# Two-layer hybrid encoder on one core: the low parts of seven split weights move from GpSimd to VectorE

## The chip, the core and the metric

The kernel runs on one core of a Trainium2 chip. A core has TensorE (PE in the profile, with PEld for its weight loads), VectorE (DVE), ScalarE (ACT), GpSimd (POOL), a queue that issues transfers (SP), and sixteen DMA engines. The metric is the device time of one execution in microseconds. The kernel before took 1442.82 us, the median of three runs (1442.33 to 1444.71).

## The reference

The input x has 256 tokens of 1024 channels in float32. After a first layer norm come two layers. Each is a mixer (one input projection, eight heads of neighbourhood attention, eight heads of sliding-window attention with two key heads and sink logits, sigmoid gates, an output projection), a residual and a layer norm, and then a channel part, a residual and a layer norm:

```
x = layer_norm(x, emb_ln_g, emb_ln_b)
for layer in range(DEPTH):
    m = mixer_block(x, w_in[layer], ...)
    x = layer_norm(DEEPNORM_ALPHA * x + m, ln1_g[layer], ln1_b[layer])
    f = swiglu(x, ...) if layer % 2 == 0 else moe_swiglu(x, w_router, ...)
    x = layer_norm(DEEPNORM_ALPHA * x + f, ln2_g[layer], ln2_b[layer])
```

The channel part of layer 0 is a dense SwiGLU of width 2816. That of layer 1 sends each token to 2 of 8 experts of width 3584.

## The kernel before

Everything up to the experts is done in three matmuls for one product: a float32 operand is split into a high part, rounded to the fp32r type, and a low part, the rest. `mm3` (L201) then adds hi·hi, hi·lo and lo·hi; these are the lines L203 to L205. Weights are split as they arrive: `load_w` (L167) transfers 128x2048 numbers (1 MB; for the first projection of a layer, `wkv`, 128x1024) into a `raw` tile, ScalarE copies them to `hi` (L185), and one engine subtracts, `lo = raw - hi` (L192). That engine is `dve`, unless the list `splitters` holds an entry, which is then used up: `eng = splitters.pop() if splitters else dve`.

The activations are split where one layer norm feeds the next product. I call such a place a meeting. There are three of them before the experts:

- the first: the embedding norm feeds the mixer of layer 0 (0 to 45 us of the trace);
- the second: the first norm of layer 0 feeds the dense SwiGLU (180 to 210 us);
- the third: the second norm of layer 0 feeds the mixer of layer 1 (380 to 412 us).

At a meeting the two halves of 128 tokens, t = 0 and t = 1, are done one after the other. VectorE adds the residual (L280), takes the statistics (L216, L217), and normalises (L224, L225). TensorE transposes (L255). ScalarE and VectorE scale half of the channels each into `xTf` (L265, L263). VectorE rounds to `xTh` (L272, two casts of 128x512) and subtracts to `xTl` (L273, two of 128x512). The matmuls of the next product then start on t = 0, and the transposes of t = 1 stand among them (`rest`). Meanwhile GpSimd works on the residual copy of x: `ln_apply` multiplies each half by the norm's gain (L234, 128x1024) once its transposes have been read, and adds the bias (L237).

The order of the instructions on each engine is set when the kernel is built, by a scheduler that estimates times, except in the stretches marked `manual_schedule`, which keep the order of the code. So a changed engine for one instruction can also change the order around it. The experts, from 594 us on, stream 896 KB and 1 MB pieces of unsplit weights into all free weight tiles (`rooms`), so transfers run ahead until the rooms are full.

Of the kernel before, what the change touches and what calls it, by code (L numbers as in the profile page):

```python
# [65 lines left out]
def tile_encoder(ctx: ExitStack, tc: tile.TileContext, x_in, emb_g, emb_b, w_in, b_gate, na_rpb, sw_sink,  # L66
# [3 lines left out]
    pe, act, dve, pool = nc.tensor, nc.scalar, nc.vector, nc.gpsimd  # L70
# [9 lines left out]
    def mm_bank():  # L80
        return pp.tile([128, 512], F32, tag="mm", name="mm")
# [61 lines left out]
    splitters = []  # L143
# [58 lines left out]
    def mm3(o, lh, ll, rh, rl, first, last):  # L202
        pe.matmul(o, lh, rh, start=first, stop=False)  # L203
        pe.matmul(o, lh, rl, start=False, stop=False)  # L204
        pe.matmul(o, ll, rh, start=False, stop=last)  # L205
# [80 lines left out]
    def mixer(l, xh, xl, rest, x, mp, close_attention, early):  # L286
# [9 lines left out]
        def load_cols(c0, n):  # L296
            return [load_w(win[:, kh * 4:kh * 4 + 4, c0:c0 + n], 4, n) for kh in range(2)]
# [39 lines left out]
        def ev_vna(t, ps):  # L337
            return act.activation(vna[:, t].rearrange("p h d -> p (h d)"), ps, AF.Copy)

        splitters[:] = [pool] * 3 if l else [pool,pool]  # L340
        wkv = load_cols(2048, 256)
        if l == 0:
            with tc.manual_schedule(engines={PE, ACT, DVE}):
# [229 lines left out]
    def dense_ffn(x, xh, xl, rest, fp, early):  # L573
# [6 lines left out]
        def load_gu(j):  # L580
            return [load_w(w[:, :, j * 256:(j + 1) * 256], 8, 256) for w in (wg, wu)]

        def new_h():
            return (fp.tile([128, 2, S], F32R, name="hh", bufs=4), fp.tile([128, 2, S], F32R, name="hl", bufs=4))

        def first():

            splitters[:] = [pool] * 2
            ws = load_gu(0)
            hh, hl = new_h()  # L590
            hts = []
            for t in range(2):
                tk = slice(t * 128, (t + 1) * 128)
                ps = mm_bank().rearrange("p (b s) -> p b s", b=2)
                for b, (wh, wl) in enumerate(ws):
                    with ExitStack() as es:
                        for c in range(KC):
                            if (t, b, c) == (0, 1, 2):
                                es.enter_context(tc.manual_schedule(engines={PE}))
                                out = rest()  # L600
                            mm3(ps[:, b], xh[:, c, tk], xl[:, c, tk], wh[:, c], wl[:, c], c == 0, c == 7)
                h = fp.tile([128, S], F32, name="h", bufs=3)
                with tc.issue_after(out.ins):
                    act.activation(h, ps[:, 0], AF.Silu)
                dve.tensor_mul(h, h, ps[:, 1])
                hts.append(h)
            yield hh, hl
            for t, h in enumerate(hts):
                tk = slice(t * 128, (t + 1) * 128)
                ps = mm_bank().rearrange("p (m s) -> p m s", m=4)[:, 0:2]  # L610
                for m in range(2):
                    pe.transpose(ps[:, m], h[:, m * 128:(m + 1) * 128], ident)
                act.activation(hh[:, :, tk], ps, AF.Copy)
                dve.tensor_sub(hl[:, :, tk], ps, hh[:, :, tk])
            yield
# [28 lines left out]


        steps = first()
        hs = [next(steps)]
        for j in range(1, NJ):
# [28 lines left out]
    def rest(ln, g, b):  # L677
        def part():
            out = to_xT(xt, ln, 1, *xT)
            if ln == 0:  # L680
                return lambda: ln_apply(xt, bcast(g, nc.sync), b, pool)
            hold_back(0, *out)
            ln_apply(xt, bcast(g), b, pool)
            return out[0]
        return part
# [9 lines left out]
    with tc.tile_pool(name="mix0", bufs=1) as mp:  # L695
        mixer(0, *xT, rest(0, emb_g, emb_b), xt, mp, lambda ap: pools["att0"].close(), early(1))
# [76 lines left out]
    with tc.tile_pool(name="mix1", bufs=1, reuse_waits="tile") as mp:  # L773
        mixer(1, *xT, rest(2, ln2_g[0], ln2_b[0]), xt, mp, prefetch_room, routed)
# [426 lines left out]
```

## Time and profile before

| | before |
|---|---|
| median of three runs | 1442.82 us (1442.33 to 1444.71) |
| the profiled execution | 1444.1 us, of it 1442.2 us span |
| PE busy | 1383.3 us, 96% |
| VectorE busy | 513.5 us, 36% |
| ScalarE busy | 336.3 us, 23% |
| GpSimd busy | 125.5 us, 9% |
| mean granted TensorE clock | 0.985 of full speed |
| transfers | 451.24 MB, 313 GB/s over the span |

A row of the timeline has the start in us, the duration in us, the engine, the line of the kernel, the operation, what it writes and reads with the shape, the count of like instructions in a row, and in brackets the idle time before it and what ended that. The duration of an instruction here includes time in which it has been started and stands still. The granted clock is given as a share of 2.4 GHz: 1.00 is 2.4 GHz and 0.50 is 1.2 GHz.

### The profile page before, as it was taken

What the parts mean: (1) busy time and instruction counts of PE and PEld (TensorE: products, weight loads), DVE (VectorE), ACT (ScalarE), POOL (GpSimd) and SP (SyncE); (2) the same over time, 40 slices, a digit from 0 to 9 for tenths busy, and PEclk for the clock granted to TensorE, in tenths of its full rate; (3) what the DMA queues carried; (4) which work ended last, traced back from release to release, by engine and by line L of the source; (5) the groups of instructions that cost most, each with busy time, mean ns of one, the idle gap of its engine ahead of it and who ended that gap; (6) DMA issues with size and microseconds to landing.
All of it is one profiled execution on the core that took longest, in us unless ns stands there. A gap on an engine that the chain in (4) does not pass through costs nothing. (4 is left out here: it accounts for less than half of the span.)

```text
span 1442.2 us, 26993 instructions
## 1 busy us (share of the span) xinstructions
PE 1383.3 (96%) x11875; PEld 777.2 (54%) x11875; DVE 513.5 (36%) x661; ACT 336.3 (23%) x533; POOL 125.5 (9%) x71
## 2 busy tenths in 40 slices
PE   7999989999899999899999999999999999999974
PEld 5888979999788898332333333333323233333321
DVE  8675676445687746710111201102010111101113
ACT  4566444444355662200000000000000000000000
POOL 5210051000351100500000000000000000000000
PEclk8999999999999999999999999999999999999998
DMA  8734437565466387599999999999999999999993
GB/s 288 238 117 153 154 125 245 179 190 166 142 202 180 104 339 253 207 419 419 418 405 364 366 419 418 419 419 417 419 419 419 419 419 417 420 419 418 418 420 145
DMA packets 122858, 451.24 MB, mean 313 GB/s; under 512 B 8032, under 2 KB 57568, under 8 KB 108528
## 3 DMA queue, kind: packets, MB, share of 16 engines
q1 hardware_dynamic: 120768, 442.91, 79.0%
q0 software_dynamic: 1968, 6.55, 1.5%
q8 instruction: 95, 1.56, 0.4%
q14 instruction: 27, 0.22, 0.0%
HBM read 448.38 MB, written 1.05 MB: 312 GB/s over the span
## 5 line engine op out<-in xcount | busy, mean ns | idle before, releaser
L933 PE MATMUL mm<-raw,gx 128*32 128x448 f32 x3648 | 370.4, 540 | 1.9 <-DMA raw<-in_moe_w_up_dram 1.3
L933 PEld LDWEIGHTS mm<-raw,gx 128*32 128x32 f32 x3648 | 117.1, 110 | 226.0 <-issue 209.6
L192 DVE TENSOR_TENSOR lo<-raw,hi 128x2048 fp32r<-128x2048 f32 x78 | 191.7, 2464 | 89.8 <-ACT hi L185 89.6
L962 PE MATMUL a<-raw,hT 128*32 128x512 f32 x1680 | 197.5, 594 | 11.3 <-DMA raw<-in_moe_w_down_dram 11.3
L203 PE MATMUL mm<-xTh,hi 128*128 128x256 f32 x704 | 202.3, 287 | 0.0
L205 PE MATMUL mm<-xTh,lo 128*128 128x256 f32 x704 | 200.0, 284 | 0.0
L204 PE MATMUL mm<-xTl,hi 128*128 128x256 f32 x704 | 199.7, 284 | 0.0
L933 PE MATMUL a<-raw,gx 128*32 128x448 f32 x1728 | 187.4, 540 | 0.0
L185 ACT ACTIVATE hi<-raw 128x2048 fp32r<-128x2048 f32 (+1 forms) x85 | 158.7, 1873 | 74.4 <-PE mm L204 43.2
L203 PEld LDWEIGHTS mm<-xTh,hi 128*128 128x128 f32 x704 | 134.6, 191 | 7.2 <-issue 5.4
L205 PEld LDWEIGHTS mm<-xTh,lo 128*128 128x128 f32 x704 | 134.6, 191 | 3.1 <-issue 3.1
L204 PEld LDWEIGHTS mm<-xTl,hi 128*128 128x128 f32 x704 | 134.7, 191 | 1.8 <-issue 1.5
L938 DVE TENSOR_TENSOR h<-h,mm 128x448 f32<-128x448 f32 x32 | 19.9, 621 | 304.6 <-PE mm L933 302.0
L962 PEld LDWEIGHTS a<-raw,hT 128*32 128x32 f32 x1680 | 50.8, 110 | 135.4 <-issue 102.6
L933 PEld LDWEIGHTS a<-raw,gx 128*32 128x32 f32 x1728 | 55.4, 110 | 107.6 <-issue 102.9
L937 ACT ACTIVATE h<-mm 128x448 f32<-128x448 f32 x25 | 13.6, 544 | 320.1 <-PE mm L933 320.1
L967 PE MATMUL a<-raw,hT 128*32 128x512 f32 x560 | 72.8, 592 | 0.0
L945 DVE STREAM_TRANSPOSE hT<-h 128x1344 f32<-128x1344 f32 (+1 forms) x15 | 33.6, 2239 | 105.5 <-PE a L967 54.0
L1116 POOL DMA_DIRECT2D raw<-in_ln_g_dram x1 | 0.6, 602 | 774.7 <-PE mm L933 774.7
L976 ACT ACTIVATE y<-a 128x512 f32<-128x512 f32 x8 | 4.8, 597 | 270.9 <-PE a L962 270.9
L205 PE MATMUL mm<-hi,xTl 128*128 128x256 f32 (+1 forms) x128 | 46.6, 365 | 6.8 <-DVE xTl L273 6.8
L203 PE MATMUL mm<-hi,xTh 128*128 128x256 f32 (+1 forms) x128 | 46.4, 367 | 3.8 <-DVE xTh L272 3.8
(244 smaller groups left out, 1463.8 us busy)
## 6 DMA issues: line engine op xcount, KB each, us to landing
raw<-in_moe_w_gate_dram SPq DMA_DIRECT2D x128, 896.0 KB, 17.8
raw<-in_moe_w_up_dram SPq DMA_DIRECT2D x128, 896.0 KB, 17.4
raw<-in_moe_w_down_dram SPq DMA_DIRECT2D x111, 1024.0 KB, 18.5
raw<-in_w_in_dram SPq DMA_DIRECT2D x32, 1024.0 KB, 5.8
raw<-in_ffn_w_gate_dram SPq DMA_DIRECT2D x11, 1024.0 KB, 5.3
raw<-in_ffn_w_up_dram SPq DMA_DIRECT2D x11, 1024.0 KB, 5.4
raw<-in_ffn_w_down_dram SPq DMA_DIRECT2D x11, 1024.0 KB, 5.0
raw<-in_w_out_dram SPq DMA_DIRECT2D x8, 1024.0 KB, 5.6
```

What stands on the lines that cost most here:

```text
L185: act.activation(hi[:, p], raw[:, p], AF.Copy)
L192: eng.tensor_sub(lo[:, p], raw[:, p], hi[:, p])
L203: pe.matmul(o, lh, rh, start=first, stop=False)
L204: pe.matmul(o, lh, rl, start=False, stop=False)
L205: pe.matmul(o, ll, rh, start=False, stop=last)
L933: pe.matmul(out[q * 32:q * 32 + 32], gx[:, c, s * 32:s * 32 + 32], wt[:, q * Q:(q + 1) * Q], start=c == 0, stop=c == KC - 1)
L937: act.activation(h[:, s, 0:Q], banks[0][s], AF.Silu)
L938: dve.tensor_mul(h[:, s, 0:Q], h[:, s, 0:Q], banks[1][s])
L945: dve.transpose(hT, h.rearrange("p s (f b) -> p s b f", f=32))
L962: pe.matmul(yb[0][r:r + 32], hT[s][:, m], w[:, n * 512:(n + 1) * 512], start=first, stop=last)
L967: pe.matmul(yb[1][r:r + 32], hT[2][:, m - 1 + i], wt[:, i, n * 512:(n + 1) * 512], start=j == 0 and m == 1, stop=last)
L976: act.activation(y[:, 0], yb[0], AF.Copy)
```

## The change

The two places that fill the list `splitters` now empty it. So all low parts are made by VectorE. Before, GpSimd made two of them at the first meeting (`wkv`, 128x1024 each), two at the second (the first gate and up weights of the dense SwiGLU, 128x2048), and three at the third (`wkv` twice 128x1024, and the first half of `wq`, 128x2048).

```
@@ -337,7 +337,7 @@
         def ev_vna(t, ps):
             return act.activation(vna[:, t].rearrange("p h d -> p (h d)"), ps, AF.Copy)
 
-        splitters[:] = [pool] * 3 if l else [pool,pool]
+        splitters.clear()
         wkv = load_cols(2048, 256)
         if l == 0:
             with tc.manual_schedule(engines={PE, ACT, DVE}):
@@ -585,7 +585,7 @@
 
         def first():
 
-            splitters[:] = [pool] * 2
+            splitters.clear()
             ws = load_gu(0)
             hh, hl = new_h()
             hts = []
```

GpSimd keeps its other work in its old order. On VectorE the seven subtractions take the following places. At the first meeting (181 and 187 are the two halves of `wkv`, `xTf_138` and `xTf_128` belong to t = 0, `bnrs_118` to the norm of t = 1):

```order
 L263 TENSOR_SCALAR xTf_138<-mm_133,pcol_79 128x128 x4
+L192 TENSOR_TENSOR lo_181<-raw_178,hi_180 128x1024
 L224 RECIPROCAL bnrs_118<-bnrs_118 128x1
 L225 TENSOR_SCALAR x_76<-x_76,bnmv_117,bnrs_118 128x1024
 L272 CAST xTh_99<-xTf_128 128x4x128
+L192 TENSOR_TENSOR lo_187<-raw_184,hi_186 128x1024
 L273 TENSOR_TENSOR xTl_100<-xTf_128,xTh_99 128x4x128
 L272 CAST xTh_99<-xTf_138 128x4x128
```

Two subtractions now stand between the scaling of t = 0 and its first low part.

At the second meeting the subtraction of the gate weights stands ahead of the first residual sum of t = 0 (L280). That of the up weights, 1955, is this one (1896 and 1886 are the two scaled halves of t = 0):

```order
 L216 BN_STATS bnst_1928<-x_76 128x6
 L263 TENSOR_SCALAR xTf_1896<-mm_1891,pcol_79 128x128 x4
+L192 TENSOR_TENSOR lo_1955<-raw_1952,hi_1954 128x2048
 L272 CAST xTh_1879<-xTf_1896 128x4x128
 L272 CAST xTh_1879<-xTf_1886 128x4x128
```

It stands between the scaling of t = 0 and its two casts.

At the third meeting (3746 and 3752 are the halves of `wkv`, 3665 and 3655 the scaled halves of t = 0):

```order
 L224 RECIPROCAL bnrs_3615<-bnrs_3615 128x1
 L225 TENSOR_SCALAR x_76<-x_76,bnmv_3614,bnrs_3615 128x1024
+L192 TENSOR_TENSOR lo_3746<-raw_3743,hi_3745 128x1024
 L263 TENSOR_SCALAR xTf_3665<-mm_3660,pcol_79 128x128 x4
+L192 TENSOR_TENSOR lo_3752<-raw_3749,hi_3751 128x1024
 L272 CAST xTh_3648<-xTf_3665 128x4x128
 L272 CAST xTh_3648<-xTf_3655 128x4x128
```

One stands ahead of the scaling of t = 0, which waits for the transposes, the other ahead of its casts.

A little later on VectorE (3758 is the first half of `wq`, `a2` and `a3` are the two residual sums of t = 1):

```order
 L273 TENSOR_TENSOR xTl_3649<-xTf_3655,xTh_3648 128x4x128
 L280 SCALAR_TENSOR_TENSOR x_76<-x_76,a2_1944 128x512
+L192 TENSOR_TENSOR lo_3758<-raw_3755,hi_3757 128x2048
 L216 BN_STATS bnst_3704<-x_76 128x6
 L280 SCALAR_TENSOR_TENSOR x_76<-x_76,a3_1945 128x512
```

This one stands inside the residual and norm of t = 1.

TensorE's order at the same place (3768 is the product with `wkv`, 3795 that with `wq`, both of t = 0; L255 are the transposes of t = 1):

```order
 L204 MATMUL mm_3768<-lo_3752,xTh_3648 128x256
 L205 MATMUL mm_3768<-hi_3751,xTl_3649 128x256
-L255 MATMUL mm_3804<-ident_80,x_76 128x128 x4
-L255 MATMUL mm_3814<-ident_80,x_76 128x128 x4
+L203 MATMUL mm_3795<-hi_3757,xTh_3648 128x512
 L204 MATMUL mm_3795<-lo_3758,xTh_3648 128x512
 L205 MATMUL mm_3795<-hi_3757,xTl_3649 128x512
```

The transposes of t = 1 went behind the first six matmuls with `wq`; before, five of these six came after them.

## Rows read from the trace of the kernel before

**Rows 1.** Busy time by stage: window, its length, each engine's busy time (instructions), clock, DMA.

```profile
0.00:30.00 30.00, 21.86 (x97) 15.84 (x98) 24.10 (x30) 14.53 (x22) 13.92 (x12) 0.83 0.80 282
30.00:175.00 145.00, 145.00 (x1069) 129.40 (x1069) 98.32 (x119) 86.27 (x157) 21.44 (x15) 1.00 0.53 169
650.00:1400.00 750.00, 737.16 (x7206) 246.22 (x7202) 94.19 (x127) 30.56 (x55) 1.13 (x2) 1.00 1.01 413
```

**Rows 2.** Waits of SP's queue, 540 to 640 us: total, times, longest.

```profile
SPq L199 <- PE a L933: 35.8, 9, 22.6
```

**Rows 3.** Timeline of VectorE at the second meeting.

```profile
175.41 2.28 DVE L192 TENSOR_TENSOR lo<-raw,hi 128x2048 fp32r<-128x2048 f32 x1
...
183.07 0.69 DVE L280 SCALAR_TENSOR_TENSOR x<-x,a 128x512 f32<-128x512 f32 x1 [5.04 <-PE a L205]
...
191.25 6.01 DVE L272 CAST xTh<-xTf 128x512 fp32r<-128x512 f32 x2
197.18 1.28 DVE L273 TENSOR_TENSOR xTl<-xTf,xTh 128x512 fp32r<-128x512 f32 x2
```

**Rows 4.** Timeline of GpSimd at the second meeting.

```profile
189.89 2.41 POOL L234 TENSOR_TENSOR x<-x,gb 128x1024 f32<-128x1024 f32 x1 [3.79 <-PE mm L255]
192.25 4.73 POOL L192 TENSOR_TENSOR lo<-raw,hi 128x2048 fp32r<-128x2048 f32 x1
```

**Rows 5.** Timeline of VectorE at the first meeting.

```profile
13.57 2.58 DVE L272 CAST xTh<-xTf 128x512 fp32r<-128x512 f32 x1
...
16.79 0.42 DVE L272 CAST xTh<-xTf 128x512 fp32r<-128x512 f32 x1
...
20.58 2.75 DVE L273 TENSOR_TENSOR xTl<-xTf,xTh 128x512 fp32r<-128x512 f32 x1
...
24.40 15.51 DVE L192 TENSOR_TENSOR lo<-raw,hi 128x2048 fp32r<-128x2048 f32 x5
```

**Rows 6.** Timeline of GpSimd at the first meeting.

```profile
13.27 2.59 POOL L192 TENSOR_TENSOR lo<-raw,hi 128x1024 fp32r<-128x1024 f32 x1 [0.17 <-ACT hi L185]
17.87 4.91 POOL L234 TENSOR_TENSOR x<-x,gb 128x1024 f32<-128x1024 f32 x2 [2.01 <-DMA gb<-in_emb_ln_g_dram]
```

**Rows 7.** Timeline of TensorE at the first meeting.

```profile
26.74 0.50 PE L204 MATMUL mm<-lo,xTh 128*128 128x512 f32 x1 [0.24 <-DVE lo L192]
```

**Rows 8.** Timeline of TensorE at the second meeting.

```profile
197.32 0.58 PE L203 MATMUL mm<-hi,xTh 128*128 128x256 f32 x1 [2.71 <-DVE xTh L272]
198.52 0.58 PE L205 MATMUL mm<-hi,xTl 128*128 128x256 f32 x1 [0.40 <-DVE xTl L273]
...
203.99 0.28 PE L205 MATMUL mm<-hi,xTl 128*128 128x256 f32 x1
204.11 1.04 PE L255 MATMUL mm<-ident,x 128*128 128x128 f32 x8
```

**Rows 9.** Busy time by stretch at the second meeting, columns as in rows 1.

```profile
200.00:202.00 2.00, 2.00 (x11) 2.00 (x11) 1.01 (x3) 0.29 (x1) 0.00 (x0) 0.50 0.85 296
...
206.00:208.00 2.00, 1.33 (x12) 1.13 (x11) 2.00 (x4) 2.00 (x3) 1.70 (x2) 1.00 0.00 0
```

**Rows 10.** Timeline of VectorE at the third meeting.

```profile
387.21 3.87 DVE L272 CAST xTh<-xTf 128x512 fp32r<-128x512 f32 x2
391.00 5.59 DVE L273 TENSOR_TENSOR xTl<-xTf,xTh 128x512 fp32r<-128x512 f32 x2
...
400.04 0.81 DVE L225 TENSOR_SCALAR x<-x,bnmv,bnrs 128x1024 f32<-128x1024 f32 x1
...
406.73 1.28 DVE L273 TENSOR_TENSOR xTl<-xTf,xTh 128x512 fp32r<-128x512 f32 x2
```

**Rows 11.** Timeline of GpSimd at the third meeting.

```profile
388.20 7.24 POOL L192 TENSOR_TENSOR lo<-raw,hi 128x1024 fp32r<-128x1024 f32 x2
```

**Rows 12.** Timeline of TensorE at the third meeting.

```profile
396.65 0.58 PE L205 MATMUL mm<-hi,xTl 128*128 128x256 f32 x1 [5.01 <-DVE xTl L273]
...
408.54 0.28 PE L205 MATMUL mm<-hi,xTl 128*128 128x256 f32 x1
```

More of the change, by code (lines that the diff above doesn't have):

```diff
@@ L338, in ev_vna @@
             return act.activation(vna[:, t].rearrange("p h d -> p (h d)"), ps, AF.Copy)
-        splitters[:] = [pool] * 3 if l else [pool,pool]
+        splitters.clear()
         wkv = load_cols(2048, 256)
@@ L586, in first @@
         def first():
-            splitters[:] = [pool] * 2
+            splitters.clear()
             ws = load_gu(0)
```

## The prediction

> **What bounds the kernel now.** I read the busy time by stage first. Until the experts TensorE is the bound: from 30 to 175 us it is busy in 145.00 of 145.00 us while the DMA engines are half used [rows 1]. In the experts the transfers are: DMA share 1.01, and TensorE loses some 13 of 750 us [rows 1]. So what is won or lost before the experts counts only if the expert transfers start earlier or later with it. They do: the queue that issues them waits 22.6 us, and 35.8 in all, for TensorE to free a tile [rows 2]. I count the meetings' gains at full value, microsecond for microsecond.
>
> TensorE's losses before the experts lie at the meetings, and the timelines there show why. At the second one VectorE's two casts took 6.01 us [rows 3], where one cast alone takes 0.42 [rows 5]. GpSimd's gain multiplication ran from 189.89 to 192.30 and its subtraction from 192.25 to 196.98 [rows 4]. The first cast ended after the one, the second after the other. So a VectorE instruction of this kind stands still until the GpSimd instruction beside it is over. TensorE waited 2.71 us for the second cast and 0.40 more for the low part [rows 8]. At the third meeting the casts took 3.87 and the two low-part subtractions 5.59 [rows 10], beside GpSimd's two weight subtractions from 388.20 to 395.44 [rows 11], and TensorE waited 5.01 us [rows 12].
>
> The wait also costs clock. After the 2.71 us TensorE ran at 1.2 GHz (0.50 at 200 us) and was back at 2.4 GHz when 206 was reached [rows 9]. From 198.52 to the transposes at 204.11 it did 28 products of 256 columns (30 stand before the transposes in the code, two were done). At full clock they start 0.12 us apart [rows 8], 3.36 us in place of 5.59: the clock cost 2.2 us there.
>
> **The change, meeting by meeting.** A subtraction of 128x2048 costs VectorE 2.28 us [rows 3]; for 128x1024 I take half and a little, 1.2 us, an estimate. Seven of them make 4 x 1.2 + 3 x 2.28 = 11.6 us more on VectorE. What counts is where they stand.
>
> First meeting. The two subtractions (2.4 us) stand where VectorE had stood still: the cast at 13.57 took 2.58 beside GpSimd's subtraction that began at 13.27 [rows 5, 6], so 2.2 us vanish there, and about as much at the normalisation before it. I get the first split done 1 to 2 us earlier. But the two multiplications by the gain remain on GpSimd from 17.87, when their transfer lands, to 22.78 [rows 6]; VectorE's casts and subtractions of t = 1 go between and behind them, as the one that took 2.75 did [rows 5]. So the row of five weight subtractions begins at 24.4 as before, and TensorE still waits for the first of them at 26.74 [rows 7]. Value: 0. Ends: -0.4, if the last GpSimd instruction comes early, and +0.6, if VectorE gets in ahead of the first and so pushes the second behind.
>
> Second meeting. The subtraction ahead of the residual falls into 5.04 us in which VectorE waited for TensorE [rows 3]: it starts when its high part is ready, ends some 0.7 us after 183.07, and is caught up by the next residual sum, which TensorE releases later. Cost 0. The second one asks at 191.25, waits for the gain multiplication until 192.3 [rows 4], ends at 194.55. Two casts at 0.42 give 195.4, two low parts at 1.28 [rows 3] give 196.65. Before, these ended at 198.46. Gain 1.8 us. TensorE, done with the old products at 197.32 - 2.71 = 194.6, now waits twice, about 0.8 us for the high part and 0.9 for the low. Does the clock fall? The trace has two waits of that size: between 206 and 210 TensorE waited twice, in 206 to 208 it was busy 1.33 of 2.00, and the clock stayed at 1.00 [rows 9]. The 2.71 us wait was one piece and cost the clock. By the nearer row it stays: another 2.2 us, so -4.0. Ends: -1.8 (it falls) and -4.1. The split of t = 1 follows with the same distances, so its two short waits stay as they are.
>
> Third meeting. The subtraction before the scaling falls into the wait for the transposes: 0. The next asks at about 387.2, waits for the gain multiplication until 388.2, ends at 389.4; casts 390.25, low parts 391.55, in place of 391.00 + 5.59 = 396.59. TensorE's 5.01 us wait goes altogether. But then t = 1 is late. Before, 11.42 us passed from 396.59 to the end of t = 1's low parts at 408.01 [rows 10]. The third subtraction stands in that chain and adds 2.28: 391.55 + 11.42 + 2.28 = 405.25. TensorE took up this part at 408.54, without waiting [rows 12]. If it now waits for it, the gain is 408.54 - 405.25 = 3.3 us: of the 5 us won, VectorE's added subtraction takes back most of the rest.
> There is a new wait on the way. The normalisation of t = 1 ends at 400.85 before [rows 10], 4.26 after 396.59; now at 391.55 + 4.26 + 2.28 = 398.1. TensorE, from 391.6, has 22 products with `wkv` at 0.12 (2.6 us) and, since the transposes moved behind them, six with `wq` of twice the columns (1.4 us, an estimate from the same pace), and is done at 395.9 if the third subtraction (ready at 391.55 + 0.69 for the residual sum [rows 3] + 2.28 = 394.5) does not hold it. So it stands 2.2 us before the transposes, in one piece. Queued behind them are the other 18 products with `wq`. The row nearest to this wait is the 2.71 us one, which cost the clock and 2.2 us [rows 8]. TensorE would otherwise be ready for t = 1 at 398.1 + 0.8 (transposes) + 18 x 0.23 + 0.6 (high part of t = 1, second `wq` half) = 403.6 to 404.3, so 1 us of the 2.2 is hidden and 1.2 counts. Value: -3.3 + 1.2 = -2.1; ends -3.3 (clock stays) and -1.0 (a longer slow stretch).
>
> Sum: 0 - 4.0 - 2.1 = -6.1 us. Against the profiled execution, 1444.1 (1442.2 of span), that is 1438.0; it lay 1.3 above the median of the runs, 1442.82. I take the median as the base and round the gain to 6: 1436.8 us.
>
> **The rivals.**
>
> The clock falls anyway. Its state depends on when a wait falls, and the two waits of the second meeting add up to 1.7 us, between the waits that cost it (2.71) and those that did not. Then the second meeting brings 1.8 and the third 2.1: 1442.8 - 3.9 = 1438.9.
>
> Nothing arrives. If the expert transfers were paced from elsewhere than TensorE's start, the gain before would turn into a longer wait in them: 1442.8. For it: DMA share 1.01. Against it: the 22.6 us for which the queue waits on TensorE [rows 2].
>
> VectorE becomes what TensorE waits for: slower. At the first meeting it is busy 24.10 of the first 30 us [rows 1]. If its long casts have another cause than GpSimd's subtractions, no stall goes, and each subtraction in a chain between norm and split counts: 1.2 + 1.2 at the first, 2.28 at the second, 1.2 + 2.28 at the third, 8.2 us, so 1451.0. It decides from the point where the casts of t = 0 at the second meeting still take over 2 us with no GpSimd instruction beside them. Against it: casts and GpSimd instructions end together, twice [rows 3, 4], and a cast alone takes 0.42. The Trainium skill has a rule for this side: its page "Perfetto Trace Analysis" (Optimizing Scalar/DVE Operations) says that with VectorE saturated, handing work even to GpSimd may make sense. By that rule the change goes the wrong way at the first meeting, the one place where the row shows a nearly full VectorE. The same section warns that the two engines share a read port, so that moving work between them might not help; there the trace agrees, with 6.01 us for two casts of 0.42.
>
> **How the numbers follow.** Forecast (both later meetings gain, with the ends above) 0.69: 1434.9 to 1439.9. The clock falls anyway 0.15: 1438 to 1440.5. Nothing arrives 0.09: 1441.5 to 1444. Slower 0.07: up to 1451. The range of 8 in 10 leaves out the slower rival and half of the case that nothing arrives: 1434.0 to 1441.9; its low end adds the first meeting's -0.4 and the -3.3 of the third with the full clock to the forecast, some 1.6 us, and 1 us for a run whose clock falls less than the profiled one. A measurement of this kernel can tell 0.2%, 2.9 us, from no change: faster is below 1439.9. That is 0.67 of the forecast's 0.69 and 0.11 of the second case's 0.15: 0.78. Same: 0.02 + 0.04 + 0.08 = 0.14. Slower: 0.08.
>
> **What would show it.** Right: the casts of t = 0 together under 1 us at the second and third meeting; TensorE's 5.01 us wait gone, and a new one of about 2 us for the normalisation (L225) before the transposes of t = 1 at the third; 1.00 of clock just after the second meeting; first expert matmul about 6 us earlier than before. Wrong: a wait over 1 us for a low part of weights (L192) anywhere, or casts that stay long without GpSimd; or an earlier expert start with an unchanged end.

## The result, and the profile after

The changed kernel took 1435.14 us (median of four runs, 1432.50 to 1437.59), the kernel before 1443.76 beside it: ratio 0.994, 95% interval 0.9922 to 0.9958. In a second comparison (after_again, below) it took 1436.95 against 1443.79, ratio 0.9957 (0.9939 to 0.9975). The twelve executions of the changed kernel have their median at 1436.0; the prediction was 1436.8, faster.

The profiled run was the longest of its four, 1437.59 us with a span of 1435.8, so 6.4 below the span before. Stages and the transfer queue's largest wait on TensorE, in the columns of [rows 1, 2]:

```profile
0.00:30.00 30.00, 21.00 (x92) 15.22 (x93) 23.63 (x32) 14.11 (x22) 8.81 (x10) 0.83 0.82 287
650.00:1400.00 750.00, 736.00 (x7182) 245.35 (x7174) 94.20 (x127) 30.56 (x55) 1.13 (x2) 1.00 1.01 413
```

```profile
SPq L199 <- PE a L933: 41.3, 12, 22.5
```

The expert stage is what it was; the queue still waits 22.5 us for TensorE. The gain was made ahead of it. The first expert matmul, before and after:

```profile
593.92 1.72 PE L933 MATMUL mm<-raw,gx 128*32 128x448 f32 x8
```

```profile
587.63 1.72 PE L933 MATMUL mm<-raw,gx 128*32 128x448 f32 x8
```

At the second meeting, VectorE and GpSimd (answering [rows 3, 4]):

```profile
182.76 2.29 DVE L192 TENSOR_TENSOR lo<-raw,hi 128x2048 fp32r<-128x2048 f32 x1 [3.41 <-ACT hi L185]
...
192.44 3.32 DVE L192 TENSOR_TENSOR lo<-raw,hi 128x2048 fp32r<-128x2048 f32 x1
195.69 0.75 DVE L272 CAST xTh<-xTf 128x512 fp32r<-128x512 f32 x2
196.36 1.28 DVE L273 TENSOR_TENSOR xTl<-xTf,xTh 128x512 fp32r<-128x512 f32 x2
```

```profile
191.22 2.40 POOL L234 TENSOR_TENSOR x<-x,gb 128x1024 f32<-128x1024 f32 x1 [86.33 <-PE mm L255]
```

The casts take 0.75 us instead of 6.01. The subtraction now ahead of them takes 3.32, for 1 us of which it stands until GpSimd's multiplication is over at 193.62. TensorE and its clock there (answering [rows 8, 9]):

```profile
196.49 0.38 PE L203 MATMUL mm<-hi,xTh 128*128 128x256 f32 x1 [0.56 <-DVE xTh L272]
...
197.69 0.39 PE L205 MATMUL mm<-hi,xTl 128*128 128x256 f32 x1 [0.70 <-DVE xTl L273]
...
201.15 1.04 PE L255 MATMUL mm<-ident,x 128*128 128x128 f32 x8
```

```profile
200.00:202.00 2.00, 2.00 (x20) 2.00 (x19) 0.58 (x1) 0.15 (x1) 0.00 (x0) 1.00 0.28 91
```

Two short waits, and the clock stays at 2.4 GHz (1.00). At the third meeting, VectorE and then TensorE (answering [rows 10, 12]):

```profile
386.31 0.75 DVE L272 CAST xTh<-xTf 128x512 fp32r<-128x512 f32 x2
386.98 1.28 DVE L273 TENSOR_TENSOR xTl<-xTf,xTh 128x512 fp32r<-128x512 f32 x2
...
388.78 2.28 DVE L192 TENSOR_TENSOR lo<-raw,hi 128x2048 fp32r<-128x2048 f32 x1
...
393.78 0.81 DVE L225 TENSOR_SCALAR x<-x,bnmv,bnrs 128x1024 f32<-128x1024 f32 x1
...
400.47 1.28 DVE L273 TENSOR_TENSOR xTl<-xTf,xTh 128x512 fp32r<-128x512 f32 x2
```

```profile
394.65 1.82 PE L255 MATMUL mm<-ident,x 128*128 128x128 f32 x8 [2.06 <-DVE x L225]
...
402.02 0.28 PE L205 MATMUL mm<-hi,xTl 128*128 128x256 f32 x1
```

The 5.01 us wait is gone. The new one, for the normalisation behind VectorE's added subtraction (388.78), is 2.06 us. Busy time by stretch shows the half clock behind it:

```profile
396.00:398.00 2.00, 2.00 (x8) 1.61 (x7) 2.00 (x3) 1.22 (x4) 1.45 (x1) 0.50 0.00 1
398.00:400.00 2.00, 2.00 (x10) 1.66 (x9) 2.00 (x4) 0.00 (x0) 1.92 (x1) 0.93 0.51 95
```

It ends soon after 398, where the clock is at 0.93 on the mean.

### The profile page after: what moved, and what is told of

Its sections match the earlier page's. It is cut to its first block, busy times and chain, and to the rows that moved or that the text cites. A ratio compares the mean times of both kernels' runs of the same rounds, so it can differ in the third digit from the quotient of the medians.

```text
span 1435.8 us, 26988 instructions
## 1 busy us (share of the span) xinstructions
PE 1380.6 (96%) x11875; PEld 774.8 (54%) x11875; DVE 511.5 (36%) x668; ACT 336.4 (23%) x533; POOL 100.6 (7%) x64
## 5 line engine op out<-in xcount | busy, mean ns | idle before, releaser
L192 DVE TENSOR_TENSOR lo<-raw,hi 128x2048 fp32r<-128x2048 f32 (+1 forms) x85 | 203.7, 2400 | 93.8 <-ACT hi L185 93.5
L962 PE MATMUL a<-raw,hT 128*32 128x512 f32 x1680 | 197.5, 594 | 12.3 <-DMA raw<-in_moe_w_down_dram 12.2
## 6 DMA issues: line engine op xcount, KB each, us to landing
raw<-in_moe_w_gate_dram SPq DMA_DIRECT2D x128, 896.0 KB, 17.7
```

Of the source, the lines that this page charges most:

```text
L192: eng.tensor_sub(lo[:, p], raw[:, p], hi[:, p])
L962: pe.matmul(yb[0][r:r + 32], hT[s][:, m], w[:, n * 512:(n + 1) * 512], start=first, stop=last)
```

## The experiments

Twelve runs. Where a gain is given in us it is the difference of the medians of that comparison, and the interval is that of the ratio.

**One meeting at a time.** In the kernel before, GpSimd is handed the subtractions by `splitters[:] = [pool] * 3 if l else [pool,pool]` in the mixers and `[pool] * 2` in the dense block. Each kernel empties the list at one meeting (the new lines only):

```diff
# first_only           splitters[:] = [pool] * 3 if l else []
# third_only           splitters[:] = [] if l else [pool,pool]
# second_only, dense:  splitters.clear()
```

> VectorE makes the two low parts of the first meeting; at the second and third GpSimd makes them as before. Theory (GpSimd instructions hold up VectorE at the meetings, and the forecast's 0 for the first meeting was right): between -0.5 and +1.5 us against before, and in the profile TensorE starts on t = 0 one to two us earlier but then waits for t = 1. Rival (the 2.6 us by which the measured gain of 8.6 exceeds the forecast of 6 come from the first meeting): -2 to -3 us.

> Only the second meeting's two low parts move to VectorE. Theory: -4.2 us against before (about 1.9 from the waits, 2.3 from a clock that no longer falls; in a run whose clock falls all the same -1.9). Rival (the added 2 x 2.28 us on VectorE take the gain back, so the whole comes from elsewhere): within 1 us of before.

> Only the third meeting's three low parts move to VectorE. Theory: -3.3 to -3.8 us against before if the clock stays up or falls only shortly, with a new wait of about 2 us of TensorE before the transposes of t = 1 in place of the 5 us wait. Rival (the forecast's value, with a full slow stretch after the new wait): -2.1 us. The three single kernels should add up to the whole change, -8.6, if the meetings are independent.

Measured against 1444.69: first_only 1442.32, ratio 0.998 (0.9966 to 0.9994); second_only 1442.20, 0.9981 (0.9966 to 0.9996); third_only 1439.92, 0.997 (0.9956 to 0.9984). The sum, -9.6 us, agrees with the whole (-8.6 and -6.8) within these wide intervals. first_only is not decided: its median lies by the rival's -2 to -3 us, but in its profile the attention begins only 0.65 us sooner (47.77 for 48.42) and the experts 1.1 later (595.04 for 593.92). third_only gave a little more than expected, -4.8, of which its profile shows 4.0 at the meeting. Another 0.8 us appear at its second meeting, where it changes nothing. TensorE there, the wait and the transposes of t = 1:

```profile
197.24 0.39 PE L203 MATMUL mm<-hi,xTh 128*128 128x256 f32 x1 [2.72 <-DVE xTh L272]
...
203.25 1.04 PE L255 MATMUL mm<-ident,x 128*128 128x128 f32 x8
```

The wait is that of the kernel before (2.72 for 2.71 us), but the granted clock was at 0.50 only from about 198.1 to 201.5, where before it was so from 196.6 to 203.4. From the transposes of t = 0 to those of t = 1, 14.57 us passed for 15.35. So the cost of the clock behind one and the same wait differs between executions.

second_only shows in its profile the 4.27 us across its meeting (its third meeting's transposes begin at 379.47 instead of 384.73, 0.99 of it from an earlier start). Yet its median gained 2.5 us, with an interval (-4.9 to -0.6) that holds the expected -4.2 as well, and its profiled execution, 1446.37 us, lay 4.2 above its median. That one lost the time later, where the routing meets the experts, a fourth place that I had not looked at (`gx` are the gathered activations that the first expert matmuls read, `turn` and `v` are small tables of the routing). VectorE, GpSimd and TensorE there:

```profile
589.48 1.12 DVE L868 TENSOR_SCALAR gx<-a,pcol 128x256 f32<-128x256 f32 x2
590.52 1.79 DVE L795 TENSOR_TENSOR v<-v,w 128x2 f32<-128x2 f32 x1
...
592.32 3.38 DVE L826 TENSOR_SCALAR turn<-turn_rk 128x6 f32<-128x6 f32 x4
595.62 0.53 DVE L868 TENSOR_SCALAR gx<-a,pcol 128x256 f32<-128x256 f32 x1
```

```profile
589.94 4.66 POOL L237 TENSOR_TENSOR x<-x,gb 128x1024 f32<-128x1024 f32 x2 [3.38 <-DMA gb<-in_ln_b_dram]
```

```profile
596.21 1.72 PE L933 MATMUL a<-raw,gx 128*32 128x448 f32 x8 [3.94 <-DVE gx L868]
```

And VectorE and GpSimd of the changed kernel at the same place:

```profile
588.10 0.38 DVE L826 TENSOR_SCALAR turn<-turn_rk 128x6 f32<-128x6 f32 x4
588.39 0.54 DVE L868 TENSOR_SCALAR gx<-a,pcol 128x256 f32<-128x256 f32 x1
588.85 2.04 DVE L826 TENSOR_SCALAR turn<-turn_rk 128x6 f32<-128x6 f32 x2
```

```profile
588.43 4.70 POOL L237 TENSOR_TENSOR x<-x,gb 128x1024 f32<-128x1024 f32 x2 [3.81 <-DMA gb<-in_ln_b_dram]
```

Even instructions of six elements a partition stand still beside GpSimd's addition of the bias. In the changed kernel the last gx gets in 0.04 us ahead of it; in second_only the bias had landed sooner (GpSimd waited 3.38 us for it, not 3.81), small instructions stood still first, and TensorE waited 3.94 us for gx. So part of the spread from run to run can be decided there by one transfer; the runs without a profile don't show it.

**GpSimd beside VectorE's unchanged order.** Both kernels are the changed kernel with one more job for GpSimd at the second meeting (shortened: shapes and the order behind the copy are left out):

```diff
+        if spare is not None:                       # beside_read
+            pool.tensor_sub(spare, raw, hi)
+            mark = pool.tensor_copy(mark, hi[:, 0, 0:1])   # beside_fill instead
+            for v in (0.0, 1.0, 2.0):
+                pool.memset(spare, v)
```

> The changed kernel, in which GpSimd, at the second meeting, in addition subtracts the up weights as it did before, into a spare tile that nobody reads: VectorE still makes every low part that is used, and the order on VectorE, TensorE and ScalarE is that of the changed kernel. Theory (a GpSimd subtraction holds VectorE's casts beside it, which is what the change took away): the casts of the first token tile before the transposes end late again, at about 200.5 us instead of 196.4, TensorE reads the low part near 202.5 instead of 197.7, and the run is 5 to 7 us longer than the changed kernel (about 1440 to 1442 in the same comparison). Rival (what helped was the order of VectorE's own work, GpSimd holds nobody): within 1 us of the changed kernel, casts end at 196.4 as there.

> As the last one, but in place of the subtraction GpSimd copies one element and then fills the spare tile three times with a constant (128x2048 each): it writes and reads no large tile. Theory (only a GpSimd instruction that reads from SBUF holds up a subtraction on VectorE with two inputs, while any holds up a one-input cast): subtractions at 1.28 us as in the changed kernel, the casts of the high part, 0.75 us there, several us: time between the changed kernel and the last one, +1 to +5 us. Rival 1 (any GpSimd instruction holds both): as the last one, +5 to +7 us. Rival 2 (a fill holds nobody): within 1 us of the changed kernel.

Measured against 1445.17: beside_read 1442.62, ratio 0.9985 (0.9969 to 1.0001); beside_fill 1440.69, 0.9975 (0.9956 to 0.9994). With VectorE's order unchanged, most of the changed kernel's gain (ratios 0.994 and 0.9957) is gone in beside_read, and by the ratios about half in beside_fill, whose interval overlaps that of after_again. VectorE, GpSimd and TensorE of beside_read:

```profile
193.59 0.75 DVE L277 CAST xTh<-xTf 128x512 fp32r<-128x512 f32 x2
194.26 5.59 DVE L278 TENSOR_TENSOR xTl<-xTf,xTh 128x512 fp32r<-128x512 f32 x2
```

```profile
193.97 4.73 POOL L197 TENSOR_TENSOR spare<-raw,hi 128x2048 f32<-128x2048 f32 x1 [2.45 <-issue]
```

```profile
199.90 0.58 PE L210 MATMUL mm<-hi,xTl 128*128 128x256 f32 x1 [5.00 <-DVE xTl L278]
```

The casts, which began first, keep their 0.75; the low parts behind them take 5.59. I had expected the casts to be the ones held; here it was the instruction that came behind the start of GpSimd's. From the last column scaling of t = 0 to the transposes of t = 1, 9.99 us pass in the changed kernel (191.16 to 201.15) and 15.59 here (189.07 to 204.66): +5.6. VectorE and GpSimd of beside_fill:

```profile
194.40 2.44 DVE L281 CAST xTh<-xTf 128x512 fp32r<-128x512 f32 x2
196.76 1.27 DVE L282 TENSOR_TENSOR xTl<-xTf,xTh 128x512 fp32r<-128x512 f32 x2
```

```profile
194.75 5.69 POOL L201 MEMSET spare<- 128x2048 f32 x3 [0.23 <-PE a L214]
```

Beside a fill, which reads nothing, the second cast stood until the first fill was over, but the subtractions took their 1.27 us while the fills went on. The Trainium skill says it so on "SBUF — State Buffer" (Who interferes with whom): a VectorE instruction with two SBUF inputs is held only by a GpSimd instruction that reads, a cast that may use both ports by any, and whoever is issued first keeps the lock for its whole instruction. These two traces agree on what is held by what. On who was first, beside_read agrees: its second cast began at 193.92, 0.05 us ahead of GpSimd's subtraction, and kept its 0.41 us. beside_fill doesn't show it: its second cast is recorded at 194.73, 0.02 us ahead of the fill, and yet it was the one held.

**The clock by itself.** The kernel before, with matmuls in place of TensorE's wait at the second meeting:

```diff
-            if l:
-                warm(8)
+            warm(8 if l else 11)
```

> The kernel before, and between the last output projection of mixer 0 and the first matmul of the dense block eleven matmuls over a tile of ones, of which nobody reads the result: TensorE works through most of the 2.71 us in which it waited for the first high part there. GpSimd keeps its subtractions. Theory (the prediction's clock term: the clock falls to half because TensorE stood still, and that alone costs 2.2 us behind the wait): the wait itself stays, the granted clock stays at 1.00, and the transposes of token tile 1 begin about 2 us sooner, near 201.9 instead of 204.1; the run about 2 us faster than before. Rival (the clock falls for another reason): half clock again after the wait, transposes at 204 as before.

TensorE of before_warm:

```profile
194.38 2.55 PE L132 MATMUL mm<-ones 128*128 128x512 bf16 x11
197.26 0.39 PE L203 MATMUL mm<-hi,xTh 128*128 128x256 f32 x1 [0.33 <-DVE xTh L272]
...
201.91 1.04 PE L255 MATMUL mm<-ident,x 128*128 128x128 f32 x8
```

The high part comes as late as before (casts of 6.03 us), but the clock stays at 1.00 and the transposes begin at 201.91 instead of 204.11. The prediction's clock term of 2.2 us is 2.20, against this profile of the kernel before; against third_only's shorter stretch of half clock behind the same wait it would be 1.4. The 2.19 us are still there at the next meeting (382.54 instead of 384.73). The whole run was not faster: 1446.93 against 1443.79, ratio 1.0013 (0.9999 to 1.0026). Its profile lost the time at the fourth place, as second_only's did: TensorE waits 4.1 us for gx and the clock falls again (0.86 from 600 to 610 us).

**The changed kernel again.**

> The changed kernel as it is, in more runs and beside those of the others. Theory (the half clock between 24 and 28 us in its first profile, which cost 1.3 us at the first meeting, comes by chance from run to run): about half of the profiles show it, and the median is 8 to 9 us below before. Rival (it belongs to the changed kernel): half clock there again, first meeting 1.3 us later than before.

1436.95 against 1443.79, ratio 0.9957 (0.9939 to 0.9975): 6.8 us, not the expected 8 to 9. The same stretch of the first meeting, in the first profile of the changed kernel and in this one:

```profile
24.00:26.00 2.00, 2.00 (x10) 1.85 (x9) 2.00 (x2) 0.00 (x0) 0.21 (x1) 0.50 0.54 204
26.00:28.00 2.00, 2.00 (x8) 1.71 (x7) 2.00 (x2) 1.31 (x3) 0.16 (x1) 0.50 0.54 109
```

```profile
24.00:26.00 2.00, 1.48 (x12) 1.16 (x11) 2.00 (x2) 0.86 (x3) 0.00 (x0) 1.00 0.72 223
26.00:28.00 2.00, 2.00 (x9) 1.63 (x10) 2.00 (x2) 2.00 (x2) 0.67 (x1) 1.00 0.55 135
```

The same program, one time with half the clock in this stretch and one time without, so it does not belong to the changed kernel; two profiles say nothing on how often. The first transposes of the attention begin at 49.73 and at 47.56, 48.42 before. The expert stage begins 6.3 and 8.6 us earlier than before, and the span ends 6.4 and 8.2 earlier.

**GpSimd's gains moved.** What still holds VectorE is GpSimd's gain and bias. They are made to wait, by a copy of one element, for a tile that VectorE writes late. gain_later does it in the changed kernel at all three meetings, before_gain_later in the kernel before (GpSimd keeps its seven subtractions). gain_last waits in the mixers for the rotary copies; gain_mix does that in mixer 0 alone and is otherwise gain_later; all_later is gain_mix with the routing's gain and bias behind gx (put together from these kernels and shortened):

```diff
+    def late_apply(seen_of, g, b):
+        mark = sp.tile([128, 1], F32, name="mark")
+        seen = pool.tensor_copy(mark, seen_of)
+        with tc.issue_after(seen.ins):
+            ln_apply(xt, g, b, pool)
...
-            ln_apply(xt, bcast(g), b, pool)
+            late_apply(xT[1][:, 3, 255:256], bcast(g), b)   # gain_last: kdup[:, 1, 1, 1, 63:64]
...
+    seen = pool.tensor_copy(mark, gx[:, 7, 255:256])        # all_later, the routing
+    with tc.issue_after(seen.ins):
+        ln_apply(xt, bcast(ln1_g[1]), ln1_b[1], pool)
```

> The changed kernel, in which GpSimd's multiplication by the norm's gain waits, by a copy of one element ahead of it, until VectorE has split t = 1; the order on VectorE, TensorE and ScalarE is that of the changed kernel. Theory (a GpSimd instruction that reads beside VectorE holds it up): the weight subtraction at the second meeting takes 2.3 instead of 3.3 us, the casts of t = 1 0.75 instead of 1.8 us, at the first meeting the 2.85 and 2.59 us become about 0.7 and 0.4; 2 us gained at the second meeting, 1 at the third, 1 to 3 at the first: -3 to -6 us against the changed kernel, -11 to -15 against before. Rival (what is left at the meetings is VectorE's own work): within 1 us of the changed kernel, -8 to -9 against before.

> The kernel before, whose GpSimd keeps its seven subtractions, with the one addition that its gain and bias multiplications at the three meetings wait until VectorE has split token tile 1 (in the changed kernel that wait was worth 2 us). Theory (gains and subtractions hold VectorE each for its own time): 2 to 4 us faster than before, near 1441, with the casts at the second and third meeting still 5 to 6 us long. Rival (the later gains are pushed against the later subtractions and nothing is won, or TensorE is late in t=1): within 1 us of before or slower.

> The changed kernel with later gains, as in gain_later, but in both mixers GpSimd's gain and bias work waits until after the rotary copies, so that it no longer stands beside the low parts of the first weights. Theory (the 1.37 and 1.38 us for which TensorE waited for a low part at the first meeting go, and about 0.5 us at the third): about 3 us faster than gain_later, near 1430.4 us. Rival (GpSimd then stands beside VectorE in the attention stage, which loses as much): within 1 us of gain_later, or slower, with the loss between 45 and 75 us.

> The changed kernel, with the gain and bias multiplications of the first meeting after the rotary copies as in gain_last, and those of the second and third after token tile 1 has been split, as in gain_later. Theory (gain_last won 2.5 us of waits for low parts and lost 2.3 us of new waits in the attention of mixer 1, which this avoids): about 2 us faster than gain_later and gain_last, a ratio to before near 0.990, no waits of 1.3 and 1.0 us between 425 and 435. Rival (the gain sits elsewhere): same as gain_last.

> gain_mix, in which the gain and bias of the fourth place, where the routing meets the experts, wait as well, until VectorE has written the last gathered activations (gx) of the first pair of experts. What is asked: in every profile so far TensorE stands 4.1 to 4.4 us there for turn_v, while small VectorE instructions that take 0.2 us elsewhere take 2.0 to 2.4 us beside GpSimd's gain; and in two profiles the last gx came behind such instructions and TensorE waited 3.9 to 4.1 us more. Theory (GpSimd's multiplications hold even VectorE's smallest instructions, as at the other meetings): the 2 us instructions before gx go, the wait for turn_v shrinks by about 4 us to under 1, and the run is 3 to 4 us faster than gain_mix, a ratio to before near 0.987. Rival (the small instructions are long for another reason, or the wait for turn_v has another last cause): the wait stays near 4 us, time as gain_mix within 1 us.

| kernel | median, us | before beside it | ratio, 95% interval |
|---|---|---|---|
| before_gain_later | 1441.49 | 1445.17 | 0.9964 (0.9946 to 0.9982) |
| gain_later | 1433.39 | 1444.69 | 0.9922 (0.9904 to 0.9941) |
| gain_last | 1432.81 | 1445.17 | 0.9911 (0.9892 to 0.9930) |
| gain_mix | 1428.96 | 1443.79 | 0.9894 (0.9875 to 0.9913) |
| all_later | 1422.92 | 1443.12 | 0.9852 (0.9824 to 0.9880) |

gain_later gave what was expected against before, -11.3 us; against the changed kernel the two ratios make it -2.6 to -5.0, where -3 to -6 was expected. At the first meeting two waits for a low part of weights are new, in TensorE's timeline:

```profile
24.00 0.50 PE L204 MATMUL mm<-lo,xTh 128*128 128x512 f32 x1 [1.37 <-DVE lo L192]
...
28.41 0.50 PE L204 MATMUL mm<-lo,xTh 128*128 128x512 f32 x1 [1.38 <-DVE lo L192]
```

before_gain_later gained, but my expectation of its casts was wrong: they took 4.30 us at the second meeting and 1.93 at the third, not 5 to 6. At the third, with the gain out of the queue, GpSimd's first two subtractions ran from 382.62 to 387.80, mostly before the casts. GpSimd's queue as a whole held VectorE, not the subtractions alone. gain_last cut the waits for low parts from 3.1 to 0.6 us and bought waits of 1.31 and 1.01 in mixer 1's attention; against gain_later it is not told apart. gain_mix has neither, and its ratio is 0.003 lower than gain_later's, with intervals that overlap a little.

For all_later, first gain_mix at the fourth place, VectorE and TensorE:

```profile
571.05 2.34 DVE L796 TENSOR_TENSOR rt_tmp<-oh,lg 128x16 f32<-128x16 f32 x1
...
573.63 2.06 DVE L796 TENSOR_TENSOR rt_tmp<-oh,lg 128x16 f32<-128x16 f32 x1
```

```profile
576.23 0.55 PE L870 MATMUL a<-Sp,xth 128*128 128x256 f32 x1 [4.21 <-DVE turn_v L839]
```

and all_later:

```profile
569.78 0.17 DVE L796 TENSOR_TENSOR rt_tmp<-oh,lg 128x16 f32<-128x16 f32 x1
...
570.20 0.18 DVE L796 TENSOR_TENSOR rt_tmp<-oh,lg 128x16 f32<-128x16 f32 x1
```

```profile
570.91 0.36 PE L870 MATMUL a<-Sp,xth 128*128 128x256 f32 x1 [0.16 <-DVE turn_v L839]
```

The theory holds, and the gain of 6 us over gain_mix is more than its 3 to 4. From mixer 1's attention to the first expert matmul the profile is 6.0 us shorter: 4.05 are the wait for turn_v, 0.63 a wait behind the two-input comparison L760 (2.07 us there, 1.44 here, beside another GpSimd subtraction, which began sooner). The other 1.3 are clock: behind the 4.21 us wait gain_mix ran at 0.50 (from 575 us on), and from the first of sixteen matmuls of L870 to the first expert matmul it took 3.68 us; all_later stayed at 1.00 and took 2.37. all_later is the best version, 1.5% below the kernel before; by the two ratios of the changed kernel it is 0.9 to 1.1% below that.

## Why the prediction was right

The mechanism was the one predicted, and so was the size as a whole. The sum was -6.1 us; the two profiles give -6.4 and -8.2 of span, the two comparisons -8.6 and -6.8. That the first profile comes so near is in part luck: there the first meeting lost 1.3 us that the sum did not have, and the third won 1.1 more than it had.

- *First meeting, 0 (ends -0.4 and +0.6).* Measured +1.3 and -0.9: outside both ends, on both sides. Of this +0.25 and -0.33 were there already at the first norm (L217 at 9.49 and 8.91, 9.24 before), ahead of the first moved subtraction. The row of low parts began at 24.01 and 23.51, near the predicted 24.4. What I put at nothing is the clock: between 10 and 34 us TensorE ran at 0.50 for 10.2 us before (12.3 to 22.5), for 10.2 in the first profile (12.6 to 16.0 and 22.8 to 29.6) and for 3.4 in the second (14.3 to 17.7). The late stretch of the first profile came with waits of 2.27 and 1.06 us for the split of t = 1; the second profile had 1.32 and 1.06 there and stayed at 1.00.
- *Second meeting, -4.0.* -4.27 and -4.26, taken from the first transposes of the attention to those of t = 1 here (155.69 us before, 151.42 and 151.43 after). By these profiles the wait's part is 2.1 us (1.8 predicted) and the clock's 2.1 (2.2 predicted). Both terms hold: beside_read puts a wait back with one GpSimd instruction (5.00 us, for the low part), before_warm gives back the clock alone, 2.20 us. The clock's part rests on a kernel before whose clock was at half for 6.8 us; against third_only's 3.4 us of it the meeting would be worth 0.8 us less. The rival that the clock falls anyway did not come at this meeting.
- *Third meeting, -2.1 (ends -3.3 and -1.0).* -3.2 and -3.3, from these transposes to those of mixer 1's attention (223.43 us before, 220.26 and 220.11 after). This is the mis-sized term, in both its parts. The wait for the normalisation came near the predicted size (2.06 for 2.2 us; the prediction's own terms, 391.6 + 2.6 + 1.4, end at 395.6 and not at 395.9, which would have made it 2.5), and the clock fell, but only for some 3.4 us (about 394.85 to 398.3), half as long as in the stretch that I had priced it by (196.6 to 203.4). In third_only the same wait of 2.06 us did not cost the clock, and the meeting gave 4.0: so the clock cost 0.7 to 0.8 us in place of 1.2, and without it the meeting is worth 4.0 in place of 3.3. VectorE's chain for t = 1 was 0.5 us shorter than I had added it up (its low parts end at 401.75; 405.25 less the 2.96 won before is 402.29).
- *Counted at full value.* Right: of what was won ahead of the experts (6.3 and 8.6 us) 6.4 and 8.2 arrived at the end. It need not: second_only and before_warm lost theirs at the fourth place in their profiles.
- *VectorE becomes what TensorE waits for.* The point named for it did not come: with no GpSimd instruction beside them the casts took 0.75 us, and VectorE's busy time fell, from 513.5 to 511.5 us, although it makes seven subtractions more. So it did in the first 30 us, where it was nearly full: 24.10 before, 23.63 after, with two subtractions more. A busy share that holds such standing still is no measure of how full an engine is.
- *"Nothing arrives"* is out by both comparisons.

What stays open: what decides whether the clock falls at a wait of about 2 us, and for how long behind a longer one; what the two subtractions of the first meeting are worth by themselves; and how often the runs without a profile lost time at the fourth place.

## What to carry to other kernels

Here work on GpSimd was free only where VectorE was not on the way to the engine that bounds: look for VectorE instructions that are several times longer than their like and end with a GpSimd instruction, and count the wait and the clock it costs behind them. Before moving work to VectorE or away, ask whether the GpSimd work can simply be later; here that, added to the change, was worth more than the change itself. And where a gain does not arrive, search the stage boundaries behind it for the same pair.

## What the runs showed of the hardware

- A GpSimd copy of one element took 4.98 us in gain_later (201.93 to 206.91), beside VectorE's subtractions (three in a row, 201.78 to 206.86), and 0.18 to 0.22 elsewhere in gain_last and all_later: GpSimd is held by VectorE as well, and being small did not protect it.

```profile
201.93 4.98 POOL L679 COPY mark<-xTl 128x1 f32<-128x1 f32 x1 [99.38 <-DVE xTl L273]
```

- VectorE instructions of 16 elements a partition stand as long as large ones: 2.0 to 2.4 us for 0.17 to 0.18, until the GpSimd multiplication beside them is over (gain_mix against all_later, L796).
- One piece of waiting of 2.71 us cost TensorE its clock, waits of 0.56 and 0.70 us close together did not, and one of 2.20 (beside_fill) did, and one of 2.06 did in two profiles (after, after_again) and did not in a third (third_only). Behind waits of 2.71 and 2.72 us the half clock lasted 6.8 us in the profiles of before and first_only and 3.4 in that of third_only.
